# Sixteen accumulating transfers behind one timing copy, and the first channel mixer's group of four with its products in another order

## The chip, the cores and the metric

The kernel runs on one core of a Trainium2 chip. The metric is the device time of one execution in microseconds (us), the median of several; less is better. A core has five instruction streams that run side by side and meet at semaphores: TensorE (PE: matmuls, with its weight loads shown as PEld), VectorE (DVE), ScalarE (ACT), GpSimd (POOL) and SyncE (SP, which here only issues transfers). Each works its stream off in order, so an instruction that waits holds up everything behind it on its engine.

## The reference

A decoder trunk of two layers on 1024 tokens of width 1024, all in float32. Layer 0 mixes tokens by a short gated convolution, layer 1 by windowed attention; each is followed by a SwiGLU channel mixer. The change touches layer 0 only, but for one constant.

```python
def short_conv_mixer(h, w_in, conv_w, w_out):
    b_gate, c_gate, xv = jnp.split(h @ w_in, 3, axis=-1)
    u = b_gate * xv
    y = lax.conv_general_dilated(u, conv_w[:, None, :], ...)   # causal, 3 taps, per channel
    return (c_gate * y) @ w_out

def swiglu_ffn(h, w_gate_up, w_down):
    g, u = jnp.split(h @ w_gate_up, 2, axis=-1)                # 1024 -> 2 x 2816
    return (jax.nn.silu(g) * u) @ w_down

def reference(x, ...):
    for i in range(DEPTH):
        h = rmsnorm(x, norm_mixer[i])
        x = x + mixer_i(h)
        h = rmsnorm(x, norm_ffn[i])
        x = x + swiglu_ffn(h, ffn_w_gate_up[i], ffn_w_down[i])
```

## The kernel before

**Products.** Each float32 operand is split into a high and a low part, and a product is three matmuls (high by high, high by low, low by high). The large matrix products are further done by a seven-product scheme on 2 x 2 blocks (Strassen's, in Winograd's form): a *unit* u is two 128-wide columns of output for all 1024 tokens, and it takes seven *kinds* k of product, 0 to 6, each of 12 matmuls of 128x512 (`three` at L1086, called from `granule_work`). Kinds 0, 1 and 4 use a block of the weights as it is; kinds 2, 3, 5 and 6 use sums of blocks (s2, s3, s1, s4). On the token side every kind has an operand of its own, made by `put`, in the tiles that `slots` names.

**Groups.** Units 0 to 3 of each large product are the *group of four*: all four units are done for one kind before the next kind begins, so a kind lasts four products. The units after them are *direct*: one after another, seven products each, with their weight sums made on DVE (L923 to L926). For the group of four the weight sums lie in DRAM and are loaded by SP (L1040).

**Sums by transfer.** For two later groups of four these DRAM sums are made by transfers alone: `sums_by_transfer` gives 16 for w_out (tile s3) and 16 for the first mixer's gate and up weights (tile s1_0), of 512 KB each, all issued on POOL's queue (L992). Of each 16, eight copy a block and eight then add a block onto one that is there (`accum_op`). To place them in time, each is issued behind a *timing copy* (L674): POOL copies one column of a tile that the convolution has just produced into a spare column of `cst`, so the transfer behind it can't start before that tile is there. The tile is one half of `sa`, the unit's buffer of partial results (tags G8 to G11), or `s3` (tags s0, s1). The first 16 transfers stand in the convolution's group of four, the last 16, all adding ones, in its direct units, behind copies after kinds 0, 2, 3 and 6. What later overwrites that half of `sa` (DVE L588 adds kind 1 to it, L644 multiplies it in place) must wait until the timing copy has read it.

**Order.** All five streams are written out by a planner: `at(t, f)` puts an instruction at a planned time, `line.work` lays the products end to end, and the streams follow those times. On PE only the order counts then; nothing waits for a clock.

**Low parts.** The split of a weight block is a cast on ACT (L1002) and a subtraction on DVE (L1003). For the pairs (k, u) in `OUT_LOWS` and `FFN_LOWS` the subtraction is a transfer instead: ACT casts (L1063), ACT writes the negated high part (L1067), and an accumulating transfer on POOL's queue adds the raw block (L1070). 256 KB each.

**The first mixer's group of four.** The convolution's output product (`second_product`, tiles Z) ends at `begin2`, and the group's first product follows at once. Its operands come from the normalised residual: `half_chain(h, t)` makes the token scales of half h (tile `rows` in the PSUM bank P2), `scale` applies them (L1268), `sum_t1` to `sum_t4` make the sums, `put` splits them. Results: kind 0 is kept in an acc bank and also starts kind 1's bank (`seeded`, L1401); SiLU of kind 1's bank goes to `sa` (L1362, for the last unit a subtraction at L1415 first); kinds 2, 3, 4 add onto kind 0's bank, 5 and 6 share a bank.

Of the kernel before, what the change touches and what calls it, by code (L numbers as in the profile page):

```python
# [13 lines left out]
ALU = mybir.AluOpType  # L14
# [53 lines left out]
MM = 0.2265  # L68
LEAD = 13.0
OUT_LOWS = [(k, u) for k in (5, 6) for u in range(GROUP)]  # L70
FFN_LOWS = [(k, u) for k in (0, 1, 2) for u in range(GROUP)]


@with_exitstack
def trunk_kernel(ctx: ExitStack, tc: tile.TileContext, xT, small, table, w_in, w_out, w_kv, w_q, w_o, w_gu, w_dn, out):
# [275 lines left out]
    def conv_layer():  # L351
# [212 lines left out]
        def unit_product(u, k, tag, direct):  # L564
# [19 lines left out]
            def sa(i):  # L584
                return units[u, "sa"][:, halves[i]]
# [10 lines left out]
            if k == 0:  # L596
# [5 lines left out]
                at(t + 0.05, f)  # L602
            if (k in (0, 2, 3, 6) if direct else k in (6, 5, 2, 3)):
                at(t + 0.8, lambda: transfer_behind(transfers, s3() if k in (5, 3) else sa(min(k, 1))))
            if k == 1:
# [65 lines left out]

        def transfer_behind(transfers, src):
            if transfers:
                pool.tensor_copy(cst[:, C_ROOM - 1 :], src[:, 0:1])  # L674
                transfers.popleft()()
# [89 lines left out]
        def second_product():  # L765
# [88 lines left out]
            for k in range(1, KINDS):  # L854
# [16 lines left out]
                ("XS0", "XS1"),  # L871
                ("A0", "A1"),
                ("XS2", "XS3"),
                ("A2", "A3"),
                ("XS4", "XS5"),
                ("A4", "A5"),
            ),
# [13 lines left out]
    class Line:  # L891
# [263 lines left out]
    def channel_mixer(layer, next_stage, src_of, operands, raw_tags, slots, line, lead_in=None, front=None):  # L1155
# [148 lines left out]
        for odd in (0, 1):  # L1304
            for p in range(4):
                at(begin2 + 0.3 + 0.01 * p if odd and front and p > 1 else t, scale, 0, 2 * p + odd)
                t_put = begin2 + 1.5 + 1.3 * p if odd and front else t + 0.8
                put(odd, p, lambda p=p, odd=odd: X[2 * p + odd][:, lo_half], t_put, sign=(-1, 1)[odd])
                t += 1.3 if odd and front else 2.4
        half_chain(1, begin2)  # L1310
        t = begin2 + 7.0
        T2 = {}
# [21 lines left out]

        for p in range(4):
            at(t, scale, 1, 2 * p)
            at(t + 0.6, scale, 1, 2 * p + 1)
            at(t + 1.2, sum_t1, p)
            at(t + 1.8, sum_t2, p)
            put(2, p, lambda p=p: T2[p // 2][:, p % 2], t + 2.4)  # L1340
            t += 2.4
        t = begin2 + 20.5
        for p in range(4):
            at(t, sum_t3, p)
            put(3, p, lambda p=p: X[2 * p][:, hi_half], t + 0.6)
            t += 2.4
        for p in range(4):
            put(5, p, lambda p=p: X[2 * p][:, lo_half], t - 0.8)
            t += 0.9
        for p in range(4):  # L1350
            at(t, sum_t4, p)
            put(4, p, lambda p=p: X[2 * p + 1][:, lo_half], t + 0.6)
            t += 2.0
        for p in range(4):
            put(6, p, lambda p=p: X[2 * p + 1][:, hi_half], t - 0.8, sign=-1)
            t += 1.0

# [6 lines left out]
        def unit_product(u, k, tag, direct):  # L1364
# [3 lines left out]
            start = k in (0, 5) or k == 1 and not seeded  # L1368
            ops_of = lambda: B[k]
            if u < GROUP:  # L1370
                srcs = {0: w_gu[layer, u][:, 0], 1: w_gu[layer, u][:, 1], 4: w_gu[layer, NF + u][:, 1]}
# [42 lines left out]
            elif k == 1:  # L1414
                at(t + 0.05, lambda: dve.tensor_tensor(sa(0), sa(0), get(), ALU.subtract))  # L1415

                at(t + (unit + 0.7 if direct else 0.8), lambda: silu(sa(0)))
            if k == 2:
                at(t + 0.05, lambda: act.copy(sa(1), get()))  # L1419
# [3 lines left out]

            if k == 3:

                def f():
                    tag = f"s{u % 2}" if u not in (2, 3) else "X0" if u == 2 else "X2"
                    units[u, "s3"] = slot(tag, (P, HALF))
                    act.copy(units[u, "s3"], get())  # L1429

                at(t + 0.05, f)
                if direct:
                    at(t + 0.75, c22)
            if k == 5 and not direct:
                at(t + 0.05, c22)
            if k == 4:

                def f():
                    H[u] = slot(("X4", "X6", "X1", "X3")[u % 4])
                    dve.tensor_tensor(H[u][:, lo_half], get(), sa(0), ALU.mult)  # L1440

                def g():
                    nc.gpsimd.dma_start(hidden[layer][u // 4][u % 2, u // 2 % 2], H[u][:, lo_half])  # L1443

                at(t + 0.05, f)
                at(t + 0.8, g)
            if k == 6:
                at(t + 0.05, lambda: dve.tensor_tensor(sa(1), get(), sa(1), ALU.add))  # L1448
                at(t + 0.8, lambda: silu(sa(1)))
                at(t + 1.6, lambda: dve.tensor_tensor(H[u][:, hi_half], units[u, "s3"], sa(1), ALU.mult))  # L1450
                if u % 2:
# [23 lines left out]
        def bank_tag(u, k):  # L1475
            if k == 1:
                return ("P0", "P1", "P3", "P0")[u]
            return "acc" if k in (0, 2, 3, 4) or u > 1 else f"P{u}"

        for k in (0, 1, 2, 3, 4, 5, 6):  # L1480
            for u in range(GROUP):
                unit_product(u, k, bank_tag(u, k), False)
# [992 lines left out]
```

## Time and profile before

| | |
|---|---|
| median of 3 runs | 1896.95 us (1896.89 to 1899.06) |
| profiled execution | 1898.37 us, of which the span of its instructions is 1896.7 us |
| granted TensorE clock, mean | 0.996 |
| PE busy | 1878.8 us of the span, 8518 matmuls |
| DVE, ACT, POOL busy | 1351.3, 871.9, 377.5 us |

The profile is one execution seen instruction by instruction. Times are us from the span's start. A busy PE is one with a matmul under way by the trace; a matmul at a lower clock is busy too, only longer, so the loss of a stretch has to be read from the number of matmuls in it and not from the busy share alone. In rows of the timeline the columns are start, duration, engine, line, operation, output <- inputs, shape, count, and in brackets the idle time just before with what ended it.

### The profile page before, as it was taken

The page shows a single profiled execution, that of the slowest core. Times are in us where ns is not written, and L with a number is a line of the kernel's source. Part 1 is how long each engine was busy: PE and PEld are TensorE (multiplying, and loading weights), DVE is VectorE, ACT ScalarE, POOL GpSimd, SP SyncE. Part 2 cuts the span into 40 slices and gives each one's busy share as a digit, 9 for nine tenths or more (in the row PEclk, how much of TensorE's full clock was granted, in tenths as well). Part 3 has the DMA queues.
Part 4 walks back from the last instruction along what each step waited for, and adds up shares of the span by engine and source line. Part 5 has one row for each costly group of instructions (what it writes and reads, how often), then busy time and mean ns, then how long its engine had stood idle before and what let it go on. Part 6 is the DMA issues. An engine that isn't in the chain of part 4 may idle for free.

```text
span 1896.7 us, 24889 instructions
## 1 busy us (share of the span) xinstructions
PE 1878.8 (99%) x8518; PEld 1560.3 (82%) x8518; DVE 1351.3 (71%) x2197; ACT 871.9 (46%) x1746; POOL 377.5 (20%) x700
## 2 busy tenths in 40 slices
PE   9998999999999999999999999999999999999999
PEld 7886788888888888888888888888888888888887
DVE  8995797868777777676677888567767666765543
ACT  5542356743333334344566777445333333344441
POOL 0132102212222322000015776400111111100000
PEclk9999999999999999999999999999999999999999
DMA  8776657756666666987741114844454654587563
GB/s 311 236 224 154 122 190 190 185 174 205 214 226 221 228 211 213 354 299 267 232 150 32 25 32 150 319 170 143 146 189 150 220 183 163 163 289 258 198 228 102
DMA packets 173312, 368.18 MB, mean 194 GB/s; under 512 B 17216, under 2 KB 63680, under 8 KB 173056
## 3 DMA queue, kind: packets, MB, share of 16 engines
q1 hardware_dynamic: 138240, 255.78, 40.6%
q0 software_dynamic: 34656, 110.64, 18.8%
q8 instruction: 67, 1.10, 0.2%
q14 instruction: 61, 0.50, 0.1%
q10 hardware_dynamic: 288, 0.16, 0.0%
HBM read 261.26 MB, written 115.87 MB: 199 GB/s over the span
## 4 chain that ended last, share of the span: by engine, by line
PE 94%; DVE 3%; issue 2%; POOL 1%; ACT 0%; POOLq 0%; DVEq 0%; ACTq 0%
PE acc L1086 48%; PE P L1086 28%; PE P L1803 2%; PE P L1805 2%; PE P L1804 2%; PE twin L2030 2%; PE acc L179 1%; PE acc L2110 1%; PE P L1212 1%; PE P L1213 1%; PE P L1211 1%; PE acc L1211 1%; PE acc L1212 1%; PE acc L1213 1%; PE acc L2079 1%
## 5 line engine op out<-in xcount | busy, mean ns | idle before, releaser
L1086 PE MATMUL acc<-XS,G 128*128 128x512 f32 x2568 | 607.1, 391 | 13.1 <-ACT G L611 8.6
L1086 PEld LDWEIGHTS acc<-XS,G 128*128 128x128 f32 x2568 | 485.2, 189 | 115.0 <-ACT G L611 9.1
L1086 PE MATMUL acc<-A,G 128*128 128x512 f32 x1674 | 395.4, 389 | 0.0
L1086 PEld LDWEIGHTS acc<-A,G 128*128 128x128 f32 x1674 | 314.3, 188 | 65.3
L1086 PE MATMUL P<-XS,G 128*128 128x512 f32 x1320 | 311.7, 389 | 0.0
L1086 PEld LDWEIGHTS P<-XS,G 128*128 128x128 f32 x1320 | 247.8, 188 | 51.7 <-ACT G L1362 0.2
L1086 PE MATMUL P<-A,G 128*128 128x512 f32 (+1 forms) x1164 | 273.5, 388 | 0.1
L1086 PEld LDWEIGHTS P<-A,G 128*128 128x128 f32 x1164 | 217.8, 188 | 45.5 <-DVE G L588 0.5
L1003 DVE TENSOR_TENSOR G<-WL,G 128x512 fp32r<-128x512 f32 x168 | 115.8, 690 | 78.3 <-ACT G L1002 77.9
L1002 ACT CAST G<-WR 128x512 fp32r<-128x512 f32 (+1 forms) x210 | 126.9, 605 | 66.7 <-PE acc L1086 27.8
L1003 DVE TENSOR_TENSOR G<-WR,G 128x512 fp32r<-128x512 f32 (+1 forms) x210 | 142.2, 677 | 8.7 <-ACT G L1002 8.7
L1002 ACT CAST G<-WH 128x512 fp32r<-128x512 f32 (+1 forms) x168 | 101.1, 602 | 83.0 <-PE acc L1086 31.6
L1002 ACT CAST G<-WL 128x512 fp32r<-128x512 f32 x168 | 103.6, 617 | 68.2 <-DVE WL L924 63.1
L1003 DVE TENSOR_TENSOR G<-WH,G 128x512 fp32r<-128x512 f32 (+1 forms) x168 | 113.3, 674 | 7.2 <-ACT G L1002 7.1
L1362 ACT ACTIVATE G<-G 128x512 f32<-128x512 f32 x48 | 30.4, 632 | 154.5 <-DVE G L1448 154.5
L1559 DVE TENSOR_TENSOR X<-X,acc 128x512 f32<-128x512 f32 x39 | 26.7, 686 | 87.4 <-PE acc L1086 87.4
L951 POOL DMA_DIRECT2D s<-X x48 | 36.6, 763 | 252.2 <-DVE X L926 124.8
L1443 POOL DMA_DIRECT2D h<-X x44 | 24.5, 558 | 251.4 <-DVE X L1440 244.2
L1429 ACT COPY s<-acc 128x512 f32<-128x512 f32 x40 | 23.5, 587 | 98.3 <-PE acc L1086 98.3
L1448 DVE TENSOR_TENSOR G<-P,G 128x512 f32<-128x512 f32 x40 | 27.6, 689 | 42.2 <-PE P L1086 42.2
L1422 DVE TENSOR_TENSOR s<-P,s 128x512 f32<-128x512 f32 x40 | 27.5, 687 | 35.0 <-ACT s L1429 29.3
L1419 ACT COPY G<-acc 128x512 f32<-128x512 f32 x44 | 25.8, 587 | 57.7 <-PE acc L1086 57.7
(329 smaller groups left out, 2730.3 us busy)
## 6 DMA issues: line engine op xcount, KB each, us to landing
G<-h SPq DMA_DIRECT2D x70, 512.0 KB, 5.0
h<-X POOLq DMA_DIRECT2D x44, 512.0 KB, 5.5
X<-in_w_dn SPq DMA_DIRECT2D x80, 256.0 KB, 3.5
s<-X POOLq DMA_DIRECT2D x40, 512.0 KB, 3.8
WR<-in_w_gu SPq DMA_DIRECT2D x36, 512.0 KB, 5.7
WH<-in_w_gu SPq DMA_DIRECT2D x36, 512.0 KB, 6.5
h<-X POOLq DMA_DIRECT2D x66, 256.0 KB, 3.8
WR<-s SPq DMA_DIRECT2D x64, 256.0 KB, 3.4
```

What stands on the lines that cost most here:

```text
L951: nc.gpsimd.dma_start(dst[:, :, c].rearrange("s p c -> p s c"), it["s"])
L1002: lambda: act.copy(out_hi, raw),
L1003: lambda: lo_eng.tensor_tensor(out_lo, raw, plain(out_hi), ALU.subtract),
L1086: pe.matmul(ps, w[:, wp, c], x[:, xp, q], start=first and i == 0, stop=last and i == 2, skip_group_check=True)
L1211: pe.matmul(ps, hi[:, kc], xs[:, 0, c], start=k == 0, stop=False, skip_group_check=True)
L1212: pe.matmul(ps, hi[:, kc], xs[:, 1, c], start=False, stop=False, skip_group_check=True)
L1213: pe.matmul(ps, lo[:, kc], xs[:, 0, c], start=False, stop=k == n_op - 1, skip_group_check=True)
L1362: state["silu"] = act.activation(x, x if of is None else of, AF.Silu, scale=sign)
L1803: pe.matmul(ps, x[:, 0, t], hi, start=k == 0, stop=False)
L1804: pe.matmul(ps, x[:, 0, t], lo, start=False, stop=False)
L1805: pe.matmul(ps, x[:, 1, t], hi, start=False, stop=k == NK - 1)
L2030: pe.matmul(ps, q, k, start=e == 0, stop=e == 1)
```

## The change

It does two things.

First, in the convolution: the direct units issue no transfers of sums any more. The first 16 transfers stay in the group of four behind 16 copies. The last 16 are issued in one run behind a single timing copy, after kind 0 of the first direct unit (`u == GROUP and k == 0`).

Second, in the first channel mixer's group of four (`front`): the kinds go 0, 1, 5, 6, 2, 3, 4 instead of 0 to 6. The operands are made in that order, at new planned times; kind 5 is copied to `s3` and 6 to `sa(1)`, and kinds 2 and 3 add to these. Kinds 5 and 6 use the banks P1, P3, P0, P2 for units 0 to 3 (before: P0, P1 and two acc banks), in the down product too. Low parts by transfer are those of kinds 0, 1, 5 and 6 (16, before 12 of kinds 0, 1 and 2). The tiles of kinds 2 and 6 are swapped (A4, A5 and A0, A1). The second half's token scales are planned 0.6 us later (`LATE`), in layer 1 also.

```diff
+LATE = 0.6
+T6_AT = 17.0
+T2_AT = 29.0
+T3_AT = 40.0
+T4_AT = 51.0
-FFN_LOWS = [(k, u) for k in (0, 1, 2) for u in range(GROUP)]
+FFN_LOWS = [(k, u) for k in (0, 1, 5, 6) for u in range(GROUP)]
...
-            if (k in (0, 2, 3, 6) if direct else k in (6, 5, 2, 3)):
-                at(t + 0.8, lambda: transfer_behind(transfers, s3() if k in (5, 3) else sa(min(k, 1))))
+            if not direct and k in (6, 5, 2, 3):
+                at(t + 0.8, lambda: transfer_behind(s3() if k in (5, 3) else sa(1), 1))
+            if u == GROUP and k == 0:
+                at(t + 0.8, lambda: transfer_behind(sa(0), 16))
...
-        def transfer_behind(transfers, src):
-            if transfers:
-                pool.tensor_copy(cst[:, C_ROOM - 1 :], src[:, 0:1])
+        def transfer_behind(src, n):
+            pool.tensor_copy(cst[:, C_ROOM - 1 :], src[:, 0:1])
+            for _ in range(n):
                 transfers.popleft()()
...
             slots=(
                 ("XS6", "XS7"),
                 ("XS0", "XS1"),
-                ("A0", "A1"),
+                ("A4", "A5"),
                 ("XS2", "XS3"),
                 ("A2", "A3"),
                 ("XS4", "XS5"),
-                ("A4", "A5"),
+                ("A0", "A1"),
             ),
...
-                t_put = begin2 + 1.5 + 1.3 * p if odd and front else t + 0.8
+                t_put = begin2 + 2.6 + 1.4 * p if odd and front else t + 0.8
...
-        half_chain(1, begin2)
-        t = begin2 + 7.0
+        half_chain(1, begin2 + LATE)
+        t = begin2 + LATE + 7.0
...
+        if front:
+            for p in range(4):
+                at(t, scale, 1, 2 * p)
+                at(t + 0.7, sum_t1, p)
+                put(5, p, lambda p=p: X[2 * p][:, lo_half], t + 1.3)
+                t += 2.0
+            t = begin2 + T6_AT
+            for p in range(4):
+                at(t, scale, 1, 2 * p + 1)
+                put(6, p, lambda p=p: X[2 * p + 1][:, hi_half], t + 1.3, sign=-1)
+                at(t + 1.7, sum_t2, p)
+                t += 2.1
...
+                if k == 5:
+                    def f():
+                        units[u, "s3"] = X[2 * u - 4][:, lo_half] if u > 1 else slot(f"s{u}", (P, HALF))
+                        act.copy(s3(), get())
+                    at(t + 0.05, f)
+                if k == 6:
+                    at(t + 0.05, lambda: act.copy(sa(1), get()))
+                if k == 2:
+                    at(t + 0.05, lambda: dve.tensor_tensor(sa(1), get(), sa(1), ALU.add))
+                    at(t + 0.8, lambda: silu(sa(1)))
...
+            if front and k in (5, 6):
+                return ("P1", "P3", "P0", "P2")[u]
             return "acc" if k in (0, 2, 3, 4) or u > 1 else f"P{u}"
...
-        for k in (0, 1, 2, 3, 4, 5, 6):
+        for k in (0, 1, 5, 6, 2, 3, 4) if front else range(KINDS):
             for u in range(GROUP):
                 unit_product(u, k, bank_tag(u, k), False)
```

POOL's stream before, from the last transfer of the group of four on (`s3` and `s1_0` are the two DRAM tiles of sums; G and s names are the tiles that the timing copies read):

```order
L992 DMA s1_0_124<-in_w_gu 128x2x512
L674 COPY cst_2_64<-G11_206_1316 128x1
L992 DMA s3_126<-in_w_out 128x2x512
L674 COPY cst_2_64<-G11_206_1316 128x1
L992 DMA s3_126<-in_w_out 128x2x512
L674 COPY cst_2_64<-s0_216_1403 128x1
L992 DMA s3_126<-in_w_out 128x2x512
L674 COPY cst_2_64<-G8_218_1423 128x1
```

The copies and transfers go on alternating like this through the direct units. POOL's stream after, at the same place, up to the next instructions of another kind:

```order
L999 DMA s1_0_124<-in_w_gu 128x2x512
L680 COPY cst_2_64<-G11_206_1316 128x1
L999 DMA s3_126<-in_w_out 128x2x512 x4
L999 DMA s3_126<-s3_126 128x2x512 x4
L999 DMA s1_0_124<-in_w_gu 128x2x512 x4
L999 DMA s1_0_124<-s1_0_124 128x2x512 x4
L849 DMA xres0_108<-A2_301_2076 128x512
```

Fifteen timing copies are gone, and with them every read of `sa` and `s3` by POOL after the first direct unit's kind 0; the transfers themselves and their order are the same.

PE's stream before, in the first mixer's group of four, from the last two products of kind 1 to the second of kind 2 (two rows to a product, the token operand's two tiles):

```order
L1086 MATMUL P3_446_2990<-XS0_430_2911,G0_436_2932 128x512 x6
L1086 MATMUL P3_446_2990<-XS1_431_2912,G0_436_2932 128x512 x6
L1086 MATMUL P0_462_3092<-XS0_430_2911,G3_443_2967 128x512 x6
L1086 MATMUL P0_462_3092<-XS1_431_2912,G3_443_2967 128x512 x6
L1086 MATMUL acc2_425_2890<-A0_449_3000,G6_447_2992 128x512 x6
L1086 MATMUL acc2_425_2890<-A1_450_3001,G6_447_2992 128x512 x6
L1086 MATMUL acc3_434_2924<-A0_449_3000,G7_453_3022 128x512 x6
```

and after, at the same place:

```order
L1093 MATMUL P3_446_2973<-XS0_431_2903,G0_436_2914 128x512 x6
L1093 MATMUL P3_446_2973<-XS1_432_2904,G0_436_2914 128x512 x6
L1093 MATMUL P0_463_3073<-XS0_431_2903,G3_443_2948 128x512 x6
L1093 MATMUL P0_463_3073<-XS1_432_2904,G3_443_2948 128x512 x6
L1093 MATMUL P1_467_3100<-XS4_448_2981,G6_447_2976 128x512 x6
L1093 MATMUL P1_467_3100<-XS5_449_2982,G6_447_2976 128x512 x6
L1093 MATMUL P3_471_3126<-XS4_448_2981,G7_452_3003 128x512 x6
```

Kind 5 now follows kind 1, and its units write the banks P1, P3, P0 and P2, of which the first three held kind 1 a moment before.

More of the change, by code (lines that the diff above doesn't have):

```diff
@@ L1333, in sum_t4 @@
             dve.tensor_tensor(b21, b21, T2[p // 2][:, p % 2], ALU.subtract)
[L1335 to L1356, printed above, removed]
+        if front:
[10 more added lines that the diff above has]
+                t += 2.1
+            t = begin2 + T2_AT
+            for p in range(4):
+                put(2, p, lambda p=p: T2[p // 2][:, p % 2], t + 0.6)
+                t += 2.2
+            t = begin2 + T3_AT
+            for p in range(4):
+                at(t, sum_t3, p)
+                put(3, p, lambda p=p: X[2 * p][:, hi_half], t + 0.6)
+                t += 2.2
+            t = begin2 + T4_AT
+            for p in range(4):
+                at(t, sum_t4, p)
+                put(4, p, lambda p=p: X[2 * p + 1][:, lo_half], t + 0.6)
+                t += 2.2
+        else:
+            for p in range(4):
+                at(t, scale, 1, 2 * p)
+                at(t + 0.6, scale, 1, 2 * p + 1)
+                at(t + 1.2, sum_t1, p)
+                at(t + 1.8, sum_t2, p)
+                put(2, p, lambda p=p: T2[p // 2][:, p % 2], t + 2.4)
+                t += 2.4
+            t = begin2 + 20.5
+            for p in range(4):
+                at(t, sum_t3, p)
+                put(3, p, lambda p=p: X[2 * p][:, hi_half], t + 0.6)
+                t += 2.4
+            for p in range(4):
+                put(5, p, lambda p=p: X[2 * p][:, lo_half], t - 0.8)
+                t += 0.9
+            for p in range(4):
+                at(t, sum_t4, p)
+                put(4, p, lambda p=p: X[2 * p + 1][:, lo_half], t + 0.6)
+                t += 2.0
+            for p in range(4):
+                put(6, p, lambda p=p: X[2 * p + 1][:, hi_half], t - 0.8, sign=-1)
+                t += 1.0
@@ L1369, in unit_product @@
             ops_of = lambda: B[k]
+            second = front and not direct
             if u < GROUP:
@@ L1417, in unit_product, with f @@
                 at(t + (unit + 0.7 if direct else 0.8), lambda: silu(sa(0)))
-            if k == 2:
+            if second:
+                s3 = lambda: units[u, "s3"]
+                if k == 5:
[8 more added lines that the diff above has]
+                    at(t + 0.8, lambda: silu(sa(1)))
+                if k == 3:
+                    def f():
+                        H[u] = slot(("X4", "X6", "X1", "X3")[u % 4])
+                        dve.tensor_tensor(H[u][:, hi_half], s3(), sa(1), ALU.mult)
+                    at(t + 0.05, lambda: dve.tensor_tensor(s3(), get(), s3(), ALU.add))
+                    at(t + 0.8, f)
+            elif k == 2:
                 at(t + 0.05, lambda: act.copy(sa(1), get()))
@@ L1422, in c22 @@
                 dve.tensor_tensor(units[u, "s3"], units[u, "b"], units[u, "s3"], ALU.add)
-            if k == 3:
+            if k == 3 and not second:
                 def f():
@@ L1433, in unit_product @@
                     at(t + 0.75, c22)
-            if k == 5 and not direct:
+            if k == 5 and not direct and not second:
                 at(t + 0.05, c22)
@@ L1438, in f @@
                 def f():
-                    H[u] = slot(("X4", "X6", "X1", "X3")[u % 4])
+                    if not second:
+                        H[u] = slot(("X4", "X6", "X1", "X3")[u % 4])
                     dve.tensor_tensor(H[u][:, lo_half], get(), sa(0), ALU.mult)
@@ L1446, in unit_product @@
                 at(t + 0.8, g)
[L1447 to L1450, printed above, removed]
+            if k == (4 if second else 6):
+                if not second:
+                    at(t + 0.05, lambda: dve.tensor_tensor(sa(1), get(), sa(1), ALU.add))
+                    at(t + 0.8, lambda: silu(sa(1)))
+                    at(t + 1.6, lambda: dve.tensor_tensor(H[u][:, hi_half], units[u, "s3"], sa(1), ALU.mult))
                 if u % 2:
```

## The prediction

> **What bounds the kernel now.** I read the page first, then PE's waits, then where in the span PE loses matmuls, and then the engines behind each of its waits. The page's busy line says that PE is the bound nearly everywhere:
>
> ```profile
> PE 1878.8 (99%) x8518; PEld 1560.3 (82%) x8518; DVE 1351.3 (71%) x2197; ACT 871.9 (46%) x1746; POOL 377.5 (20%) x700
> ```
>
> So a change that adds or drops no matmul can only win back time in which PE stands or runs slowly. PE's list of waits (engine, line, what it waited for, us in all, times, longest) has two that matter:
>
> ```profile
> PE acc L1086 <- ACT G L611: 8.6, 1, 8.6
> PE acc L1086 <- ACT s L618: 4.5, 1, 4.5
> ```
>
> Both lie in the convolution's direct units, as the busy times by stretch show (PE first, with its matmuls as x; after POOL the clock, the DMA share and GB/s):
>
> ```profile
> 100.00:150.00 50.00, 50.00 (x222) 41.40 (x221) 45.03 (x71) 21.38 (x37) 15.56 (x23) 1.00 0.68 203
> 150.00:200.00 50.00, 41.36 (x173) 33.72 (x172) 30.40 (x52) 14.77 (x26) 10.29 (x14) 0.90 0.68 145
> 200.00:250.00 50.00, 45.37 (x188) 36.67 (x187) 36.80 (x57) 15.30 (x27) 8.11 (x11) 0.93 0.61 126
> ```
>
> A full stretch of 50 us holds 222 matmuls, so one takes 0.225 us. The two stretches lack 49 and 34, which is 83 x 0.225 = 18.7 us, more than the 13.1 us of waiting; the clock column (0.90, 0.93) says that the rest is slow running. PE's timeline shows each part, product by product (12 matmuls a row):
>
> ```profile
> 172.11 2.88 PE L1086 MATMUL acc<-XS,G 128*128 128x512 f32 x12
> 174.83 2.88 PE L1086 MATMUL P<-A,G 128*128 128x512 f32 x12
> 186.36 5.38 PE L1086 MATMUL acc<-XS,G 128*128 128x512 f32 x12 [8.64 <-ACT G L611]
> 191.57 2.89 PE L1086 MATMUL acc<-A,G 128*128 128x512 f32 x12
> ...
> 230.12 2.88 PE L1086 MATMUL acc<-A,G 128*128 128x512 f32 x12
> 237.50 5.40 PE L1086 MATMUL acc<-XS,G 128*128 128x512 f32 x12 [4.50 <-ACT s L618]
> 242.75 2.92 PE L1086 MATMUL P<-XS,G 128*128 128x512 f32 x12
> ```
>
> From one start to the next a product takes 2.72 us (172.11 to 174.83). The first stall costs 186.36 - 174.83 - 2.72 = 8.81 us, and the product after it 191.57 - 186.36 - 2.72 = 2.49 us, since it runs at half speed. The second costs 237.50 - 230.12 - 2.72 = 4.66 us and 242.75 - 237.50 - 2.72 = 2.53 us. Together that is 18.5 us; the count of matmuls has 0.2 us more.
>
> Why PE stands is read from ACT and DVE. ACT's rows show that the copy which PE waits for (L611) stood in the queue behind another ACT instruction:
>
> ```profile
> 184.59 0.72 ACT L549 ACTIVATE X<-G,cst 128x512 f32<-128x512 f32 x1 [15.76 <-DVE G L644]
> ...
> 185.73 0.57 ACT L611 COPY G<-acc 128x512 f32<-128x512 f32 x1
> ```
>
> and DVE's rows what held that one:
>
> ```profile
> 183.87 0.69 DVE L644 TENSOR_TENSOR G<-s,G 128x512 f32<-128x512 f32 x1 [13.37 <-POOL cst L674]
> ...
> 232.19 0.69 DVE L588 TENSOR_TENSOR G<-P,G 128x512 f32<-128x512 f32 x1 [10.36 <-POOL cst L674]
> ```
>
> Both DVE instructions overwrite a half of `sa` that a timing copy (L674) has yet to read. The copies are late because POOL's stream stands at its transfers:
>
> ```profile
> 132.90 1.22 POOL L992 DMA_DIRECT2D s<-in_w_out  x1 [0.41 <-issue]
> ...
> 176.40 1.14 POOL L992 DMA_DIRECT2D s<-s  x1 [5.02 <-issue]
> 177.10 0.63 POOL L674 COPY cst<-G 128x1 f32<-128x1 f32 x1
> 182.49 1.15 POOL L992 DMA_DIRECT2D s<-s  x1 [4.76 <-issue]
> 183.18 0.65 POOL L674 COPY cst<-G 128x1 f32<-128x1 f32 x1
> ...
> 236.90 1.15 POOL L992 DMA_DIRECT2D s<-s  x1 [4.74 <-issue]
> 277.67 0.62 POOL L842 DMA_DIRECT2D xres<-A  x1 [39.62 <-DVE A L828]
> 300.31 0.89 POOL L1070 DMA_DIRECT2D G<-s  x1 [13.40 <-DVE A L1003]
> ```
>
> An adding transfer is issued only 6.09 us after the one before (176.40 to 182.49), and 16 of them with their copies stretch from 132.90 to 236.90. A direct unit of seven products lasts 7 x 2.72 = 19.0 us and has four copies in it, which need 24.4 us at that pace: POOL falls behind by 5 us a unit, until the copies hold DVE, DVE holds ACT, and ACT holds a PSUM bank that PE wants.
>
> **The change, part by part.** *The copies.* Fifteen of them go; the one that stays reads `sa(0)` at the point where POOL is still on time. POOL's waits then stand before nothing that DVE writes, and both stalls lose their cause: -18.5 us, and the small rest in the matmul count, say -18.7. What is late next? DVE, by its load: it was busy 30.40 + 36.80 = 67.2 us in those 100 us, and the same work now has 100 - 18.7 = 81.3 us, a load of 83%, below the 90% (45.03 of 50) of the stretch ahead, in which PE lost no matmul. The copies' own time saves nothing, as POOL isn't waited for otherwise.
>
> A rule of the Trainium skill prices the slow products otherwise. The page "TensorE: Matmul & The Clock Gate", section "What's actually happening", has the clock halved after an idle window of about 3.4 us and full again after about 3.4 us of work, so a restart would lose 1.7 us; as an estimate by that page this part would win 8.81 + 4.66 + 2 x 1.7 = 16.9 us, and the time be 1880.4. The rows agree on the halving but show it for a whole product, so their 2.49 and 2.53 stand.
>
> *The run of 16.* The transfers are the same, in the same order, from the same moment on. At 6.09 us each the last is issued at 132.90 + 15 x 6.09 = 224 us. The bounds are 1.14 us each (its own row; done by 151) and, if two at the old pace were in each other's way, twice 6.09 (done by 316, which is where rival (b) begins). POOL's next work is the store of xres, which moves with PE from 277.67 to about 259, and the first low part, from 300.31 to about 281.6. At the pace of the rows both are hidden behind 35 us of an idle POOL. Cost 0.
>
> *The group of four.* The matmuls are as many as before. DVE does four low parts fewer, ACT four negations more and POOL four transfers more; one negation is
>
> ```profile
> L1067 ACT ACTIVATE G<-G 128x512 fp32r<-128x512 f32 x20 | 12.4, 622 | 0.1
> ```
>
> so 2.5 us of ACT and no wait to speak of. PE lost nothing here before, so this part has nothing to win. What it can lose is a bank: kind 5 writes P1, P3 and P0 right after kind 1, and before the first matmul of unit u may start, the last reader of the bank must be through. In the old order kind 2 came there and wrote acc banks long free. PE's rows give the times at which kind 1 and its successor begin, ACT's and DVE's rows the last readers:
>
> ```profile
> 350.30 11.14 PE L1086 MATMUL P<-XS,G 128*128 128x512 f32 x48
> 361.27 11.04 PE L1086 MATMUL acc<-A,G 128*128 128x512 f32 x48
> ```
> ```profile
> 359.82 0.59 ACT L1362 ACTIVATE G<-P 128x512 f32<-128x512 f32 x1
> ...
> 363.51 0.58 ACT L1362 ACTIVATE G<-P 128x512 f32<-128x512 f32 x1
> ```
> ```profile
> 358.43 1.40 DVE L1268 SCALAR_TENSOR_TENSOR X<-A,cst,P 128x512 f32<-128x512 f32 x2
> ...
> 365.84 0.68 DVE L1415 TENSOR_TENSOR G<-G,P 128x512 f32<-128x512 f32 x1
> ```
>
> The readers end at 360.41 (P1), 364.09 (P3) and 366.52 (P0) even at the old engines' lag; kind 5 wants the banks at 361.27, 363.99 and 366.71. That is 0.9, -0.1 and 0.2 us of room. In the new order SiLU of P1 and of P3 stand behind fewer casts, so I expect about a microsecond more room than that. P2 holds the token scales, whose last read (L1268) was over at 359.83; now four of the eight scalings are planned some 10 us later, and unit 3 of kind 5 wants the bank at 369.4. Bounds: a gain can't come out of this (no lost matmuls before), nothing lost at best, and at worst a wait like the second stall with its slow product, 4.66 + 2.53 = 7.2 us. I take 0.3, nearest to the room that the rows show.
>
> *The end of layer 0.* With tiles A0, A1 and A4, A5 swapped, the down product's last kind now frees A0, A1 last, and attention's split of its second block of query weights (into A0) waits for the product's end. It was the second of these three casts:
>
> ```profile
> 966.96 2.96 ACT L1002 CAST A<-G 128x1024 fp32r<-128x1024 f32 x3 [0.22 <-PE acc L1086]
> ```
> ```profile
> 975.07 0.68 DVE L1003 TENSOR_TENSOR WL<-G,WL 128x512 fp32r<-128x512 f32 x1
> ```
> ```profile
> 976.55 0.39 PE L1803 MATMUL P<-WL,XS 128*128 128x512 f32 x1
> ```
>
> The cast began about 968 and can begin about 969; what stands behind it on ACT moves by 1 us. The nearest need is the low part that DVE ends at 975.75 and PE reads one matmul after 976.55, again 1 us later. So 0 to 1 us; I take 0.1.
>
> *LATE* moves both layers' second scale chain by 0.6 us, which shifts planned places but adds no instruction: 0.
>
> *Sum.* -18.7 + 0.3 + 0.1 = -18.3 us. The profiled execution took 1898.37 us (span 1896.7), so it would take 1880.1. It stood 1.4 us above the median of 1896.95; against that median I predict 1878.6 us, 1.0% faster. A difference under 0.2% (3.8 us) is about what can't be told from none.
>
> **The rivals.** (a) *The banks hold PE in the group of four.* For it: the room of -0.1 to 0.9 us above, in four products on end. Against: SiLU moves forward. One stall gives 1878.6 + 7.2 - 0.3 = 1885.5 us, still faster.
>
> (b) *The run of 16 holds POOL, slower than before.* Low parts and xres stand behind it in POOL's stream. The first of them is needed by the out product's kind 5, and one takes 5.5 us to land:
>
> ```profile
> 316.23 4.24 PE L1086 MATMUL P<-A,G 128*128 128x512 f32 x18
> ```
> ```profile
> G<-s POOLq DMA_DIRECT2D x12, 256.0 KB, 5.5
> ```
>
> Issued at 300.31, it has 316.23 - 300.31 - 5.5 = 10 us of room, so PE begins to wait when the run ends later than 281.6 + 10, a pace of (291.6 - 132.9) / 15 = 10.6 us; it eats the whole gain and 3.8 us more at (291.6 + 22.1 - 132.9) / 15 = 12.1 us, giving 1900.8 or more. Against: every adding transfer already went back to back with the next at 6.09 us, half of that.
>
> (c) *The run takes the DMA engines from SP's loads.* The DMA share in these stretches is already 0.68 and 0.61, and shorter stretches raise it to about 0.8. If the weights of three of the six direct units came late, with a stall of 7.2 us each, the gain would be gone: 1878.6 + 21.6 = 1900.2, of two 1893.0, of one 1885.8. The page "DMA: Bandwidth & Descriptors" of the Trainium skill, section "SWDGE vs HWDGE vs iDMA", speaks for it: each DMA engine takes turns between POOL's and SP's queues. No row here shows a load that PE waits for.
>
> (d) *The copies are not the cause.* If DVE were just too slow, its stalls would stay and the time with them, 1897. Against: it stood idle for 13.37 and 10.36 us.
>
> **How the numbers follow.** My forecast, both stalls gone and at most 2 us lost elsewhere, gets 0.80; (a) 0.11; (b) 0.03; (c) 0.04; (d) 0.02. The forecast's own range is 1877 to 1881. The overall range goes from 1876.5 (18.7 us won, nothing lost, and a microsecond or two of scatter such as the 2.2 us between the three runs) to 1885.5, which takes in (a) with one stall. Faster by over 0.2%: the forecast, (a) and half of (c), 0.93; within: (d) and some of (c), 0.03; slower: (b) and the rest, 0.04.
>
> **What would show it.** PE's waits without L611 and L618 rows of several us; 222 matmuls and a clock of 1.00 in every stretch of 50 us from 100 to 300; DVE's waits without the timing copy's line; 16 transfers of sums about 6 us apart on POOL, with its next work after them and not held; the group of four starting about 19 us sooner, with kind 5 following kind 1 without a gap. I am wrong if PE waits for ACT or DVE at P banks after kind 1, for a load from SP in the direct units, or for low parts whose transfers were issued late.

## The result, and the profile after

The changed kernel took 1880.27 us (median of 4 runs, 1879.21 to 1880.63); the kernel before, on the same chip, took 1897.86 us (1896.89 to 1899.06). The ratio is 0.9906, with a 95% interval of 0.9889 to 0.9923: about 17.6 us less. The profiled execution took 1880.63 us (span 1878.9); the prediction had 1880.1 for it.

The page's busy line and PE's list of waits of the changed kernel:

```profile
PE 1873.5 (100%) x8518; PEld 1556.7 (83%) x8518; DVE 1349.9 (72%) x2193; ACT 874.4 (47%) x1750; POOL 375.2 (20%) x689
```
```profile
PE P L382 <- DVE s L379: 1.1, 1, 1.1
PE acc L184 <- ACT WH L156: 0.5, 1, 0.5
PE acc L1093 <- ACT s L1486: 0.4, 1, 0.4
```

The two waits of 8.6 and 4.5 us are gone, and no wait that is left exceeds 1.1 us. The stretches of 50 us that lacked 49 and 34 matmuls are full and at full clock (PE's column first, its matmuls as x; behind POOL the clock and the DMA share):

```profile
100.00:150.00 50.00, 50.00 (x222) 41.43 (x221) 45.05 (x71) 21.34 (x37) 13.90 (x20) 1.00 0.68 204
150.00:200.00 50.00, 50.00 (x223) 41.40 (x222) 43.32 (x71) 16.97 (x31) 8.02 (x7) 1.00 0.72 169
200.00:250.00 50.00, 50.00 (x222) 41.43 (x221) 40.52 (x64) 22.13 (x40) 6.87 (x6) 1.00 0.81 203
```

On PE's timeline the product that stood until 186.36 now starts 2.72 us after the one ahead, like all others. In the second fence is the instruction of DVE that waited 13.37 us for the timing copy (L644 before, L651 now): no bracket, so no wait.

```profile
175.01 2.88 PE L1093 MATMUL P<-A,G 128*128 128x512 f32 x12
177.73 2.88 PE L1093 MATMUL acc<-XS,G 128*128 128x512 f32 x12
180.45 2.88 PE L1093 MATMUL acc<-A,G 128*128 128x512 f32 x12
```
```profile
170.70 0.69 DVE L651 TENSOR_TENSOR G<-s,G 128x512 f32<-128x512 f32 x1
```

POOL's timeline shows the one copy, the run of 16, and the next work behind it:

```profile
132.48 0.18 POOL L680 COPY cst<-G 128x1 f32<-128x1 f32 x1 [11.51 <-ACT G L605]
133.07 1.21 POOL L999 DMA_DIRECT2D s<-in_w_out  x1 [0.41 <-issue]
...
153.69 1.15 POOL L999 DMA_DIRECT2D s<-in_w_out  x1 [5.00 <-issue]
163.86 1.14 POOL L999 DMA_DIRECT2D s<-s  x1 [9.03 <-issue]
...
240.42 1.15 POOL L999 DMA_DIRECT2D s<-s  x1 [9.56 <-issue]
259.67 0.62 POOL L849 DMA_DIRECT2D xres<-A  x1 [18.11 <-DVE A L835]
```

The run is as slow as single transfers were, or slower: (240.42 - 133.07) / 15 = 7.16 us from one to the next, with a few steps of about 10 us. Nothing that another engine writes waits for it any longer, and POOL still stands idle for 18 us before its next work.

The group of four on PE:

```profile
314.27 10.36 PE L1093 MATMUL acc<-XS,G 128*128 128x512 f32 x45
324.47 0.63 PE L325 MATMUL P<-G,means 128*128 128x512 f32 x2
324.94 6.32 PE L1093 MATMUL acc<-XS,G 128*128 128x512 f32 x27
331.09 21.92 PE L1093 MATMUL P<-XS,G 128*128 128x512 f32 x96
352.85 11.04 PE L1093 MATMUL P<-A,G 128*128 128x512 f32 x48
```

The 96 matmuls from 331.09 are kinds 1 and 5 without a gap between them: the banks came free in time. At 12 matmuls and 2.72 us a product, kind 5 wants P1, P3, P0 and P2 at 341.97, 344.69, 347.41 and 350.13. Their last readers are the SiLU of P1 and of P3 on ACT, and on DVE the subtraction with P0 and the last scaling with the token scales in P2:

```profile
340.09 0.59 ACT L1396 ACTIVATE G<-P 128x512 f32<-128x512 f32 x1
...
342.27 0.58 ACT L1396 ACTIVATE G<-P 128x512 f32<-128x512 f32 x1
```
```profile
345.33 0.68 DVE L1450 TENSOR_TENSOR G<-G,P 128x512 f32<-128x512 f32 x1
...
346.53 0.74 DVE L1275 SCALAR_TENSOR_TENSOR X<-A,cst,P 128x512 f32<-128x512 f32 x1
```

They end 1.3, 1.8, 1.4 and 2.9 us before the bank is wanted.

### The profile page after: what moved, and what is told of

Read it like the earlier page. It is cut to its first block, busy times and chain, and to the rows that moved or that the text cites. A ratio compares the mean times of both kernels' runs of the same rounds, so it can differ in the third digit from the quotient of the medians.

```text
span 1878.9 us, 24856 instructions
## 1 busy us (share of the span) xinstructions
PE 1873.5 (100%) x8518; PEld 1556.7 (83%) x8518; DVE 1349.9 (72%) x2193; ACT 874.4 (47%) x1750; POOL 375.2 (20%) x689
## 4 chain that ended last, share of the span: by engine, by line
PE 98%; DVE 1%; DMA 1%; issue 0%; SPq 0%; ACT 0%; DVEq 0%
PE acc L1093 48%; PE P L1093 32%; PE P L1864 2%; PE P L1865 2%; PE P L1866 2%; PE twin L2091 2%; PE acc L184 1%; PE acc L2171 1%; PE P L1219 1%; PE P L1220 1%; PE P L1218 1%; PE acc L1218 1%; PE acc L1220 1%; PE acc L1219 1%; PE acc L2140 1%; PE acc L188 1%
## 5 line engine op out<-in xcount | busy, mean ns | idle before, releaser
L1093 PE MATMUL acc<-XS,G 128*128 128x512 f32 x2478 | 581.7, 389 | 0.4 <-ACT s L1486 0.4
L1093 PEld LDWEIGHTS acc<-XS,G 128*128 128x128 f32 x2478 | 465.0, 188 | 97.5 <-ACT s L1486 0.8
L1093 PE MATMUL acc<-A,G 128*128 128x512 f32 x1584 | 374.4, 389 | 0.0
L1093 PEld LDWEIGHTS acc<-A,G 128*128 128x128 f32 x1584 | 297.4, 188 | 61.7
L1093 PE MATMUL P<-XS,G 128*128 128x512 f32 x1410 | 331.8, 389 | 0.0
L1093 PEld LDWEIGHTS P<-XS,G 128*128 128x128 f32 x1410 | 264.7, 188 | 54.9
L1093 PE MATMUL P<-A,G 128*128 128x512 f32 x1254 | 294.2, 388 | 0.0
L1093 PEld LDWEIGHTS P<-A,G 128*128 128x128 f32 x1254 | 234.6, 188 | 48.8 <-DVE s L1479 0.5
L1501 POOL DMA_DIRECT2D h<-X x44 | 24.5, 557 | 267.0 <-DVE X L1498 259.4
L1498 DVE TENSOR_TENSOR X<-acc,G 128x512 f32<-128x512 f32 x44 | 30.4, 690 | 31.0 <-PE acc L1093 31.0
L2125 ACT ACTIVATE G<-G,at_x 128x129 f32<-128x129 f32 x128 | 50.0, 395 | 4.2 <-DVE at_x L2119 3.9
```

Source lines behind the costliest of these rows:

```text
L1093: pe.matmul(ps, w[:, wp, c], x[:, xp, q], start=first and i == 0, stop=last and i == 2, skip_group_check=True)
L2125: act.activation(e[:, i], e[:, i], AF.Exp, bias=S[u]["mx"][:, i : i + 1], scale=-1.0, accum_out=den[:, i : i + 1])
```

## The experiments

The theory: the timing copies in the direct units are the whole cause, because each stands on POOL behind an adding transfer that keeps POOL for 6 to 7 us, and DVE may not overwrite `sa` until the copy has read it. The new order of kinds is worth nothing that can be measured. The rivals: the order of kinds brings part of the gain; the transfers' traffic, not the copies, delayed DVE and PE; or the copies hold DVE by their mere number and place. The kernels ran in three lots, each with the kernel before on the same chip: 1897.30, 1897.70 and 1897.59 us.

### One part at a time

`run_alone` is the kernel before with the first part of the change only, `order_alone` the changed kernel with the old copies and transfers put back.

```diff
 run_alone, to the kernel before:
-            if (k in (0, 2, 3, 6) if direct else k in (6, 5, 2, 3)):
-                at(t + 0.8, lambda: transfer_behind(transfers, ...))
+            if not direct and k in (6, 5, 2, 3):
+                at(t + 0.8, lambda: transfer_behind(..., 1))
+            if u == GROUP and k == 0:
+                at(t + 0.8, lambda: transfer_behind(sa(0), 16))
 order_alone, to the changed kernel: the same lines the other way round
```

> The kernel before with the first half of the change alone: the 16 adding transfers in one run behind one timing copy, the first mixer's group of four as before. Theory (the copies were the whole cost): both stalls of the direct units go, 19.4 us by the trace of the changed kernel between the second and the sixth product of each stall, so 1878.5 +- 1 us, and a start of the first mixer's group about 19.3 us sooner than before. Rival (the new order of kinds is needed to keep the gain, since DVE and ACT now reach the group with less slack): a new wait of 2 us or more in the group, so 1880.5 us or more.

> The changed kernel with the old transfers: timing copies and adding transfers alternate through the direct units again, the group of four stays in its new order. Theory: both stalls are back, and the group gains the 0.4 us that the changed kernel shows at the means of its second half, so 1896 to 1898 us. Rival (the order gives a good part of the gain): under 1893 us.

Measured: `run_alone` 1879.73 us (ratio 0.9909, 0.9892 to 0.9925), `order_alone` 1897.28 us (ratio 1.0001, 0.9992 to 1.0011). `run_alone` lies 0.2 us above the range that I expected for it, `order_alone` inside its own. The first part alone brings all of it, the second alone nothing. With the old copies PE's waits and DVE's rows ahead of them are those of the kernel before:

```profile
PE acc L1091 <- ACT G L616: 8.3, 1, 8.3
PE acc L1091 <- ACT s L623: 4.1, 1, 4.1
```
```profile
183.72 0.69 DVE L649 TENSOR_TENSOR G<-s,G 128x512 f32<-128x512 f32 x1 [13.05 <-POOL cst L679]
...
231.62 0.69 DVE L593 TENSOR_TENSOR G<-P,G 128x512 f32<-128x512 f32 x1 [10.00 <-POOL cst L679]
```

### Copies without the hold, and copies without the transfers

`free_copies` keeps all 16 copies and 16 transfers of the direct units in the kernel before, but the copies read `cst` and not `sa` or `s3`, so that DVE has nothing to wait for. (The transfers are then no longer held back to their places.) `copies_alone` keeps the copies as they are and leaves the 16 adding transfers out, so the sums stay incomplete.

```diff
 free_copies:
-  transfer_behind(transfers, s3() if k in (5, 3) else sa(min(k, 1)))
+  transfer_behind(transfers, cst if direct else s3() if k in (5, 3) else sa(min(k, 1)))
 copies_alone:
-                transfers.popleft()()
+                f = transfers.popleft()
+                if len(transfers) >= 16:
+                    f()
```

> The kernel before, with as many copies at the same places in POOL's stream, but the 16 of the direct units read a column of the constants tile in place of a tile that DVE overwrites. Theory (what costs is that DVE must wait until a late copy has read): both stalls go although every copy and every transfer is still there, 1878 to 1880 us. Rival 1 (the copies' number, their time or POOL's alternation with transfers costs): 1890 us or more. Rival 2 (the transfers go some 11 us sooner without timing and take DMA time from loads): a new wait for a load, 1881 us or more.

> The kernel before, with all timing copies, reading what they read before, but the last 16 transfers left out (the weight sums are then incomplete). Theory (a copy is late only because a transfer ahead of it in POOL's stream takes 6 us to issue): no copy is late, both stalls go, 1877 to 1880 us. Rival (a copy by itself delays DVE, as the two share memory ports): DVE still waits for the copies, and more than 2 us of PE's waits at L611 and L618 remain.

Measured: `free_copies` 1879.58 us (ratio 0.9908, 0.9893 to 0.9923), `copies_alone` 1879.71 us (0.9909, 0.9894 to 0.9923). Either half of the pair is harmless alone. In `free_copies` the same copies alternate with the same transfers through the same stretch, first and last row here, and no engine waits for them:

```profile
124.44 1.22 POOL L992 DMA_DIRECT2D s<-in_w_out  x1 [3.73 <-issue]
125.16 1.17 POOL L674 COPY cst<-cst 128x1 f32<-128x1 f32 x1
...
228.96 1.15 POOL L992 DMA_DIRECT2D s<-s  x1 [4.32 <-issue]
```

So neither the traffic nor the copies' number was the cause; it was a read of `sa` that came late. (The transfers ran some 8 us earlier than before, and so still beside the two places where PE had stood, at 178 and 221 us here.) In `copies_alone`, where the copies come on time, DVE's list has only this for them (16.4 us for L644 before, and 10.4 for L588, which no longer waits for a copy):

```profile
DVE G L644 <- POOL cst L674: 0.7, 2, 0.3
```

### What makes POOL slow

`plain_run` and `half_run` are the changed kernel with other transfers in the run: in the first the 16 copy and do not add (so the sums are not sums), in the second each adds in two transfers of 64 partitions, 32 of 256 KB instead of 16 of 512 KB.

```diff
 plain_run:
-            how = {"accum_op": ALU.add} if i > 3 else {}
+            how = {}
 half_run:
-                steps.append(lambda to=to[:, h], of=of[:, h], how=how: nc.gpsimd.dma_start(to, of, **how))
+                for r in (slice(0, P // 2), slice(P // 2, P)) if i > 3 else (slice(0, P),):
+                    steps.append(lambda to=to[r, h], of=of[r, h], how=how: nc.gpsimd.dma_start(to, of, **how))
...
-                at(t + 0.8, lambda: transfer_behind(sa(0), 16))
+                at(t + 0.8, lambda: transfer_behind(sa(0), 32))
```

> The changed kernel with the 16 transfers of the run as plain copies in place of adding ones (the weight sums are then wrong). Theory (adding is what makes a transfer hold POOL's stream for 6 us): they are issued under 3 us apart, as the 16 plain ones of the group of four are, and the run is over before 180 us. Rival (any transfer from DRAM to DRAM holds POOL that long when one follows another at once): about 6 us apart as before. The time stays within 2 us of the changed kernel's either way, if neither DMA traffic nor POOL bounds this stage.

> The changed kernel with each adding transfer of the run cut into two of 64 partitions: 32 of 256 KB. Theory (the pace is that of the bytes or descriptors under way: the next transfer is issued when an earlier one has nearly landed): they are issued about 3.3 us apart and the run ends near 240 us as before. Rival (a fixed time for each adding transfer): about 6.5 us apart, the run ends near 340 us, and the low parts behind it are late as in the run that begins three units later, or worse.

One execution each: 1880.14 and 1879.78 us. First and last issue of the run, `plain_run` first:

```profile
132.75 2.14 POOL L999 DMA_DIRECT2D s<-in_w_out  x3 [0.38 <-issue]
...
171.51 0.69 POOL L999 DMA_DIRECT2D s<-s  x1 [1.05 <-DMA s<-s]
```
```profile
133.26 2.99 POOL L1000 DMA_DIRECT2D s<-in_w_out  x3 [0.34 <-issue]
...
203.27 0.94 POOL L1000 DMA_DIRECT2D s<-s  x1 [1.45 <-issue]
```

Plain transfers are 38.76 / 15 = 2.58 us apart, so it is the adding that takes 7.16. Halves are 70.01 / 31 = 2.26 us apart: the same bytes are issued in 70 us instead of 107. For `half_run` both my theory (the run ends near 240) and its rival (near 340) were wrong: it ended at 203. The cut halves the bytes and the partitions of a transfer at once; which of the two counts, and why POOL's stream is held at all, these runs don't show. Neither run moves the time, since nobody waits for it.

That gives a repair that leaves every copy in its place. `half_copies` is the kernel before with halves, two behind each copy of the direct units:

```diff
-                transfers.popleft()()
+                for _ in range(1 if len(transfers) > 32 else 2):
+                    transfers.popleft()()
```

> The kernel before with its timing copies where they stood; only each adding transfer of the direct units is cut into two of 64 partitions, both issued behind the same copy. Theory (the copies hold DVE only because an adding transfer of 512 KB keeps POOL's stream for 6 us or more, and two of 256 KB keep it for 4.5): four copies a unit need 18.1 us, less than the unit's 19.0, so POOL does not fall behind, no instruction of DVE waits for a timing copy for more than a microsecond or two, PE shows no wait of several us in the direct units and the time is 1879 to 1881. Rival (a copy in the unit holds DVE by its mere place, or the pace is set by the bytes): two halves take what one whole took, the two stalls stay and the time is 1895 to 1898.

Measured: 1879.76 us (ratio 0.9907, 0.9892 to 0.9922), with the last transfer issued at 209.20 (236.90 before), and DVE's wait down to this:

```profile
DVE G L644 <- POOL cst L674: 1.1, 2, 0.8
```

The copies may stand where they stood, as long as POOL keeps up with them.

### Where the run would cost

`late_run` begins the run three units later; `late_half` does the same with halves.

```diff
-            if u == GROUP and k == 0:
+            if u == GROUP + 3 and k == 0:
```

> The changed kernel with the run of 16 begun three direct units (57 us) later. At the changed kernel's pace of 6.7 us on the mean the run then ends near 190 + 107 = 297 us, 14 us after the first low part of the out product is due on POOL (282.7). Theory (POOL's cover ends there): the low parts land about 10 us late, PE waits in the out product's kind 5 for 4 to 10 us and runs one product slowly after it, 1885 to 1894 us. Rival 1 (the cover is deeper than reckoned, as the ring of weights holds eight products): no loss, 1880 us. Rival 2 (the run itself goes faster when it meets fewer loads): it ends by 285 us, no loss.

> The run of 16 begun three units late as in late_run (which ended its last transfer at 296 us and took 1892.8 us), with each adding transfer cut into two of 64 partitions. Theory (late_run lost its time only because the low parts stood behind the run on POOL): at 2.3 us for each of 32 the run ends at about 260 us, ahead of the first low part, PE shows no wait at the out product's kind 5 and the time is 1879.5 to 1881. Rival (the lateness of the sums, or their traffic beside the low parts' loads, cost it): 1888 or more.

`late_run`: 1892.80 us (1891.64 to 1895.26; ratio 0.9975, 0.9965 to 0.9986). PE's wait, and POOL's rows from the last transfer of the run on:

```profile
PE P L1093 <- DMA G<-s: 11.6, 1, 11.6
```
```profile
296.35 1.15 POOL L999 DMA_DIRECT2D s<-s  x1 [8.47 <-DMA WH<-s]
297.04 2.18 POOL L849 DMA_DIRECT2D xres<-A  x3
304.65 0.56 POOL L849 DMA_DIRECT2D xres<-A  x1 [5.44 <-issue]
305.19 1.81 POOL L1077 DMA_DIRECT2D G<-s  x2
```

The low parts (L1077), which in the changed kernel begin at 282.69, stood behind the run until 305.19, and PE wanted the first at 298. That is the mechanism of the prediction's rival (b), but not its price. (b) let PE wait for a run that ends later than 291.6; this one was last issued at 296.35, 4.75 us later, and PE waited 11.57 us. What (b) left out are the four stores of xres, which had piled up behind the run and stand ahead of the low parts: from the run's last issue to the first low part they take 305.19 - 296.35 = 8.84 us. By these rows the point lies near 296.35 - 11.57 = 284.8 (an estimate, which takes the stores to need as long behind a run that ends a little earlier).

`late_half` was to undo that, and did not: 1888.64 us (1887.27 to 1891.31; ratio 0.9957, 0.9943 to 0.9971). The run did end early, at 255.76, and no low part is waited for. PE waits at another place, 260 to 270, at the start of the convolution's output product:

```profile
PE P L1094 <- DVE A L835: 5.9, 1, 5.9
...
PE P L1094 <- ACT G L1010: 0.7, 1, 0.7
```

Behind both stand ACT's casts of the weights that SP loads: DVE stood 4.98 us until the second of the casts below, and from there on it worked without a gap until the L835 that PE waited for. ACT's rows (the second names PE, but see its load below), and DVE's:

```profile
252.04 0.62 ACT L1010 CAST G<-WH 128x512 fp32r<-128x512 f32 x1 [4.84 <-DMA WH<-in_w_out]
...
259.51 0.62 ACT L1010 CAST G<-WR 128x512 fp32r<-128x512 f32 x1 [5.81 <-PE P L1094]
```
```profile
260.16 0.69 DVE L1011 TENSOR_TENSOR G<-WR,G 128x512 fp32r<-128x512 f32 x1 [4.98 <-ACT G L1010]
```

The load of that WR was issued at 242.09, and the trace's answer for this one transfer is

```profile
DMA to landing us min/median/max: 17.3/17.3/17.3
```

so it landed at 259.4, right before the cast. In `half_run`, where the run was over by then, no load into WR from 228 to 262 took more than 8.3 us. The windows of `late_half`, and after them those of `half_run`, show the DMA engines (share in the last column but one; a packet counts where it starts, so the share can pass 1):

```profile
240.00:250.00 10.00, 10.00 (x46) 8.29 (x45) 7.39 (x12) 2.06 (x4) 3.44 (x4) 1.00 1.08 304
250.00:260.00 10.00, 9.51 (x42) 7.53 (x41) 2.49 (x4) 2.15 (x4) 2.23 (x3) 1.00 1.07 286
```
```profile
240.00:250.00 10.00, 10.00 (x46) 8.29 (x45) 9.91 (x17) 4.99 (x9) 0.00 (x0) 1.00 0.63 225
250.00:260.00 10.00, 10.00 (x45) 8.29 (x45) 9.71 (x16) 3.50 (x7) 0.62 (x1) 1.00 0.36 108
```

From 228 to 240 SP issues eight loads of the residual, 512 KB each, besides the weights. The run in halves beside them keeps the engines full until 260, and the weights come late; matched matmul by matmul, PE lost 9.0 us there. In `late_run` whole transfers ran beside the same eight loads: there no load into WR from 226 to 262 took more than 11.4 us, and PE lost nothing before the low parts. My theory for this run was wrong, and the rival that put the loss on traffic held, though the loads that came late were SP's weights and not the low parts. The page "DMA: Bandwidth & Descriptors" of the Trainium skill, section "SWDGE vs HWDGE vs iDMA", has each DMA engine take turns between the queues; the trace agrees so far as POOL's transfers did slow SP's loads, but the order of single packets was not read.

### The rest of the order of kinds

`late_front` is the changed kernel with the 0.6 us (`LATE`) in layer 0 alone:

```diff
-        half_chain(1, begin2 + LATE)
-        t = begin2 + LATE + 7.0
+        late = LATE if front else 0.0
+        half_chain(1, begin2 + late)
+        t = begin2 + late + 7.0
```

> The changed kernel with the 0.6 us later scale chain in layer 0 alone, layer 1 as before. In layer 1 the changed kernel lost about 0.25 us at the means and 0.15 us a few products on, and 1.0 us in a wait near 1339 us. Theory (the later chain in layer 1 costs at the means, and the 1.0 us is the landing of a store that varies from run to run): 0.2 to 0.5 us faster than the changed kernel in the trace, not to be told in the times. Rival (the 1.0 us comes from the later chain too): the wait at 1339 us is gone in the trace, 1.4 us faster.

Measured: 1880.45 us (1880.30 to 1880.64; ratio 0.9909, 0.9894 to 0.9924): no difference in the times. In the trace the 0.2 us at layer 1's means is won, as the theory had it, and the wait near 1339 us stands, against the rival (both below). Then the run alone and the changed kernel again, on one chip:

> The kernel before with the run of 16 alone and the old order of kinds, run beside the changed kernel on one chip to tell a few tenths of a microsecond. Theory (the new order wins 0.5 us in the group of four and gives about 1 us back in layer 1): 1879.5 to 1880.0, some 0.3 to 0.8 us less than the changed kernel. Rival (what the trace shows in layer 1 is chance of one execution): the two agree within 0.2 us, or the changed kernel is the quicker by 0.5.

> The changed kernel as it is, beside the run of 16 alone on the same chip. Theory: 1880.2 to 1880.6, slower than the run alone by 0.3 to 0.8 us, with the wait of some 0.4 us for ACT's copy to s in layer 1's group of four. Rival: within 0.2 us of it or quicker.

Measured: 1879.50 us (1879.40 to 1879.75) and 1879.47 us (1878.86 to 1880.50). My expectation, that the new order costs 0.3 to 0.8 us in all, was wrong; the order of kinds is worth nothing that these runs can tell. No kernel of the study is measurably better than the changed one.

## Why the prediction was right, and where its terms were off

**The stalls: right, 0.3 us too small.** Matched matmul by matmul, PE's starts in the changed kernel are 0.18 us later than before at 174 us and 18.82 us earlier at 254, so the convolution gave 19.00 us where the prediction had 18.7. The four variants without the stalls (the changed kernel, `run_alone`, `free_copies`, `half_copies`) all give 19.0. What the term left out is, for the most part, a third, small delay in the trace of before, which PE's list of waits does not name:

```profile
202.46 2.88 PE L1086 MATMUL acc<-XS,G 128*128 128x512 f32 x12
205.47 3.06 PE L1086 MATMUL P<-A,G 128*128 128x512 f32 x12
208.36 2.88 PE L1086 MATMUL acc<-XS,G 128*128 128x512 f32 x12
```

By starts that is 208.36 - 202.46 - 2 x 2.72 = 0.46 us. With the 18.5 us of the four products it makes 18.95. `order_alone` has the delay too, the four variants without the stalls don't. The estimate by the Trainium skill's page "TensorE: Matmul & The Clock Gate", section "What's actually happening", 16.9 us for this part, was too small: the rows' own 2.49 and 2.53 us for the slow products stood. In the trace of before the granted clock is 0.50 from 186.36 to 191.48 and from 237.50 to 242.68, which is 5.1 and 5.2 us of work at half clock and not about 3.4.

**What is late next: right.** DVE was busy 43.32 + 40.52 = 83.8 us of the 100, where 83% was forecast, and PE lost no matmul.

**The run of 16: cost 0 as forecast, pace wrong.** It took 7.16 us a transfer and not 6.09, and ended at 240 instead of 224, since the two neighbouring rows that the prediction took its pace from do not hold the steps of 10 us. Its own first and last row had them: (236.90 - 132.90) / 15 = 6.93 us. The 18 us in which POOL stands idle behind it hid that.

**The group of four: the mechanism right, the sign wrong.** The banks held nobody, as forecast, with 1.3 to 2.9 us of room where the prediction's rows and its microsecond for the earlier SiLU gave 0.9 to 1.9 for the first three. But "nothing to win" was wrong by a little: from the group's first matmul to kind 1's, PE took 350.30 - 333.13 = 17.17 us before and 331.09 - 314.27 = 16.82 us after, and `run_again`, with the old order, 17.25. The 0.4 us lie at the matmuls of the second half's means, which wait less for DVE in the new order. The term was +0.3 and measured -0.4 there; by the matched starts it is -0.5 over the whole group, in `order_alone` too.

**The end of layer 0 and LATE.** By the matched starts the lead is 19.32 us at 475 us of before and still at 981, past the place of the swapped tiles, so the swap cost nothing that can be seen. From 1031 to 1190, in attention, the lead falls by 0.3 us; `copies_alone`, which has nothing of the second part, loses as much there and the second trace of the changed kernel nothing. From 1269 to 1330, at the means of layer 1's group of four, it falls by 0.2 us. All seven traces with LATE in layer 1 lose about 0.2 us there, `late_front` and the traces with the old order nothing: that is what LATE costs, where the prediction had 0. Further on in layer 1's group of four the lead falls by another 1.0 us, at a product that waits for ACT's copy behind a DVE instruction that waits for a DMA. PE's row, and DVE's:

```profile
1339.00 3.03 PE L1093 MATMUL acc<-XS,G 128*128 128x512 f32 x12 [0.40 <-ACT s L1486]
```
```profile
1334.46 0.69 DVE L1518 TENSOR_TENSOR X<-X 128x512 f32<-128x512 f32 x1 [6.01 <-DMA h<-X]
```

The second trace of the changed kernel has the wait too (0.16 us in front of that product), `late_front` has it without LATE in layer 1, `order_alone`, `half_run` and `late_half` don't have it with LATE. So LATE is not what makes it. Of the eight traces with the new order five have it, of the six with the old order (before's among them) none, and in those five DVE's wait for the DMA is 5.8 to 6.2 us instead of 4.8 or 4.9. Whether the new order makes it likelier stays open. Half a microsecond won in the group and one and a half lost later make one, less than what two runs of the same kernel differ by (1880.63 - 1879.21 = 1.42), and the times of `run_again` and the changed kernel agree to 0.03 us.

**The sum** was 18.3 us less, and 17.6 us was measured by the medians (17.8 by the spans). The matched starts make up the spans' figure: 19.0 won in the convolution and 0.5 in the group, 0.3, 0.2 and 1.0 lost in layer 1, and 0.2 by which this execution was late ahead of the first stall. The first term, 18.7 of the 18.3, was understood; that the rest came out so near is luck, since 1.2 us more gain than forecast (0.3 in the convolution, 0.8 in the group, 0.1 at the tiles) and 1.7 us of losses that were not forecast went against each other. The time itself, 1880.27, is 1.7 us above the 1878.6 of the forecast and inside its 1877 to 1881; 0.9 of that is the kernel before, whose median stands at 1897.86 beside this result and stood at 1896.95 when the forecast was made.

**The rivals.** (a) did not happen: kind 5 begins without a gap. (b) and (c) did not happen in the changed kernel. Both were shown to be real mechanisms when the run was moved: `late_run` is 12.5 us above the changed kernel's 1880.27, with (b)'s margin 7 us too wide, and `late_half` is 9.2 us above the 1879.47 of the same chip. (d) is refuted by `free_copies`, which leaves DVE's work as it was and takes away only what it waited for.

## What to carry to other kernels

A tiny instruction that is there only to time a transfer is a reader like any other: whoever overwrites what it reads waits for it, as late as the queue it stands in. When a wait names a trivial instruction, read that engine's stream ahead of it and compare the pace of what stands there with the rate at which it is asked for (here 24 us of POOL or more in each unit of 19). Before moving a long run of transfers, work out two margins, when its queue is needed next, with all that will have piled up in that queue ahead of the piece that counts, and what other loads share the DMA engines while it lasts. Here, by an estimate from `late_run`, the first begins to cost at a run that ends after about 285 us, and the second cost where a quick run met 4 MB of other loads.

## What the runs showed of the hardware that I had not expected

An adding DRAM to DRAM transfer of 512 KB keeps POOL's stream for 7.16 us on average, a plain one for 2.58, and an adding one of half the size for 2.26, less than a third of the whole one. Quicker issue is not free, though: with the halves running beside SP's loads, single weight loads took up to 17.3 us to land, against 8.3 where the halves were over by then (`half_run`).
